# One core, an encoder layer in split float32: the down projection's first weights in other tiles, and planner delays, issue orders and buffers changed at eight other places

## The chip, the cores and the metric

The kernel runs on one core of a Trainium2 chip. The metric is the device time of one execution in microseconds. Three runs of the kernel before took 2294.54, 2300.36 and 2303.19 us; their median, 2300.36 us, is the time before.

## The reference

One layer of a bidirectional encoder is applied to a prompt (1024 tokens) and a sample (256 tokens) with the same weights, D_MODEL 1024, all in float32. In order:

```python
h = rmsnorm(x, norm_mix_w)
proj = h @ w_in                      # q/k/v, decays, gates, gMLP halves
y_a = deltanet_branch(...) @ w_up_a  # conv, gated delta rule in both directions, 4 heads
y_b = spatial_gating_branch(...) @ w_up_b
x = x + (sigmoid(gate_a) * y_a + sigmoid(gate_b) * y_b) @ w_out
x = x + memory_cross_attention(rmsnorm(x), rmsnorm(mem), ...)   # 4 heads, 256 memory tokens
h = rmsnorm(x, norm_ffn_w)
gu = h @ ffn_w_gate_up               # 2 x 2816 columns
x = x + (silu(gu[..., :D_FF]) * gu[..., D_FF:]) @ ffn_w_down
y = rmsnorm(x, final_norm_w)
```

## The kernel before, in words

**Products.** Activations lie with channels on partitions and tokens along the free dimension, in three blocks of 512, 512 and 256 tokens (block 2 is the sample). Each factor is split into a high part (a copy to fp32r, on ScalarE, line 125) and a low part (the rest, a subtraction on VectorE or GpSimd, line 126); `mm3` (line 110) makes of each product three: high·high, high·low, low·high. All matrix products pass line 108, transposes line 121.

**Order of the work.** TensorE's order is that in which the program issues its products. A planner in the class `Trunk` sets it: `K.clock` counts planned nanoseconds (`mm` adds n / 2.4 for n fp32r columns). The main work is a generator that yields after every `mm3` step (three products); at each yield `pump` runs the side generators whose due time has come. A side generator's `yield 2800` means: go on when 2800 ns of planned products have been issued. `K.finish` runs a side generator to its end with no main work between. The other engines' and the DMA queues' orders are made by the tile scheduler, and each queue then runs in order. A tile of a pool with `bufs=n` may exist n times under its tag; a further one waits for the oldest.

**Norms.** `Norm.add` sums squares; `Norm.rest` (line 247) waits `lag`, sums over partitions by products with ones (`nacc`), makes the reciprocal root by eleven small VectorE operations (`nst`, lines 224 to 228, 258), yields 2800, broadcasts the roots over partitions by float32 products with the unit matrix (line 263), and scales the eight 128-channel slices, one per `pace`. Those in `shared` are scaled by ScalarE and multiplied on GpSimd (lines 271, 272). The sample's norm before the FFN takes `lag=LAGS`; the last norms are started by `last_norm` (line 1931), for block 1 after phase 5 of the down projection, for block 0 after phase 6, for the sample at the end.

**Mixer.** `decays` (line 439) computes the decays; after `yield 5000` four products with triangular matrices sum them (line 480). Four heads and the sample are five batches of `dn_batch` (line 648), side work beside the main convolutions, gates and memory projections. A batch solves its triangular systems on VectorE, waits for the previous batch's flags, sums squares of the queries (`SQ`), joins the inverse's blocks by products and transposes (`LEV`), sets the flag "inverse", and scans its chunks (`SC1` to `SC3`). When the last batch is done, `load_ya` (line 1108) loads branch A, with `yield YA` between its six pairs of loads, beside `up_b` (line 1090), whose gate loads go over the same queue.

**Attention.** `load_kv` (line 1344) loads and splits keys and values of a head through one tile `kraw`. `attend` computes scores, exponentials `e` (8 buffers), transposes and outputs.

**FFN.** The up projections of the prompt work by a Strassen-like scheme: `ff_first` (line 1698) is its first of 22 tiles. Its products take the weights `gu_w[0, 0..3]` and the activation quarters b11, b21, r1, b22, r2, t3, t4; the last three are made there on VectorE and ScalarE. `gu_gate(1)` splits the first weight of the next tile, the low part on GpSimd. The sample's products begin with the second tile (`ff_up(1)`).

The down projection of the prompt (`down_prompt`, line 1874) has seven phases of six units (one to two pairs of 128 channels). `a_prep(i)` makes the weight combination of unit i and splits it into a room from `a_room(i)` (line 1648); the rooms rotate over two pairs of the pool `wp` and one tile of the pool `ffd` (`down_room`, line 1821), which is opened only when the up projection's pools are closed. The raw weights of unit u and half e lie at `home[e][u]`; units 1 to 3 of the first phase are loaded early into other tiles, 4 and 5 by the loads of step 0 (line 1861). The unit's 12 or 24 products read the room (`ahl` in `ffd`, `whi`/`wlo` in `wp`) and the activations `bhl`, which are loaded from `gq`, where the up projection stored them.

```python
def a_room(i):
    if i % 3 < 2:
        return tuple(t.rearrange(...) for t in pair_of(wp))
    t = down_room()
    return t[:, 0], t[:, 1]
```

Of the kernel before, what the change touches and what calls it, by code (L numbers as in the profile page):

```python
# [163 lines left out]
def trunk_kernel(ctx: ExitStack, tc: tile.TileContext, a):  # L164
# [65 lines left out]
    class Norm:  # L230
# [16 lines left out]
        def rest(self, xk, wcol, sink, pace=1300, shared=(), lag=1500, ks=range(KT), inplace=False, ready=None, halves=1):  # L247
# [12 lines left out]
            yield 2800  # L260
# [178 lines left out]
    def decays():  # L439
# [37 lines left out]
        yield 5000  # L477
# [170 lines left out]
    def dn_batch(bi, qkv, chains):  # L648
# [175 lines left out]
        for level, mask in enumerate((m64, m128)):  # L824
# [21 lines left out]
            for hs in halves:  # L846
                for q, d in ((lo64, 0), (hi64, 1)):
                    S.activation(Mt[q, hs, :], U[d][q, hs, :], AF.Copy)
                yield LEV
            for hs in halves:  # L850
# [8 lines left out]
        flags.add(("inverse", bi))  # L859

# [334 lines left out]
    class OutProj:  # L1195
# [21 lines left out]
        def run(self, xsrc, scale, wcol, xpool, store, sinks=None, then=None, ready=None):  # L1217
# [23 lines left out]
            for b, (t0, n) in enumerate(BLOCKS):  # L1241
# [15 lines left out]
                if sinks is None or b == 2:  # L1257
                    norm_b = nms[b].rest(xk, wcol, to_h(hs, b), 600, lag=1500 if sinks is None else LAGS, inplace=sinks is not None, ready=ready)
# [20 lines left out]
    def attend(h, qh, ql, kh, kl, vh, vl, o_h):  # L1279
        es = {}  # L1280

        def scores(b, c):
# [12 lines left out]
            e = tp.tile([P, NMEM], F32, tag="e", name="e", bufs=8)  # L1295
# [45 lines left out]
    for h in range(HEADS):  # L1341
        qh, ql = (tq.tile([P, 2, NTOK], F32R, tag=f"q{i}", name=f"q{i}") for i in range(2))

        def load_kv():
            kv = [tp.tile([P, 1024], F32R, tag=f"kv{i}", name=f"kv{i}", bufs=2) for i in range(4)]
            for i, src in enumerate((kd[2 * h : 2 * h + 2], vd[h])):
                raw = tp.tile([P, 1024], F32, tag="kraw", name="kraw")
# [105 lines left out]
    def gu_gate(f):  # L1453
        if f < NFF:
            gu_w[f, 0] = pair_of(wp)
            split(*gu_w[f, 0], gu_raw[f][0], G)
# [63 lines left out]
    split(*gu_w[0, 2], gu_raw[0][0], V)  # L1520
    for k in range(4):
        parts(r2, k, r2_raw[k], V)
    fs = ExitStack()
# [124 lines left out]
    def a_room(i):  # L1648

        if i % 3 < 2:  # L1650
# [47 lines left out]
    def ff_first():  # L1698
# [12 lines left out]
        yield from gu_mm(pe, w(1), 1, r1, True)  # L1711
        make_t3()
        yield from gu_mm(pf, w(2), 1, b22, True)
        gu_gate(1)
        yield from gu_mm(pa, w(1), 0, r2, False)
# [95 lines left out]
    f0 = [hp.tile([P, 4, 1024], F32, tag=t, name="w0") for t in ("hi1",)]  # L1811
    f1 = [hp.tile([P, 4, 1024], F32, tag=t, name="w1") for t in ("lo1",)]
    for n, w in ((4, f0), (4, f1), (2, f0), (2, f1)):
        e = int(w is f1)
        w.append(dpool.tile([P, n, 1024], F32, tag=f"w{e}{n}", name=f"w{e}"))
    for e, w in enumerate((f0, f1)):
        for u in range(1, len(units)):
            home[e][u] = w[(u - 1) // 2], 2 * ((u - 1) % 2)
# [55 lines left out]
    def down_prompt():  # L1874
        a_prep(2)
# [4 lines left out]
        for ph, (key, more, half, b, sign) in enumerate(STEPS):  # L1880
# [20 lines left out]
            for u, pairs in enumerate(units):  # L1901
# [13 lines left out]
                if i == 1:  # L1915
                    pair_home(1)
                    SY.dma_start(home[1][0][0], w_dn[1][:, units[0], :])
                a_prep(i + 3)
# [12 lines left out]
    def last_norm(nm, b):  # L1931
# [5 lines left out]
        K.side(nm.rest(lambda k: x2[b][:, k, :], S_FIN, sink, PACEF, SHARED[b], LAGF[b]))  # L1937
# [84 lines left out]
SQ, EXP, LEV = 1000, 4000, 500  # L2022
SC1, SC2, SC3 = 1200, 700, 700
TAIL, ROOT, FIRST_EXP = 3000, (2500, 2500, 2500, 16000, 2500), 3500
YA = 3000
# [3 lines left out]
LAGS, FIRST_W = 19000, 9000  # L2029
# [83 lines left out]
```

## Time and profile before

| what | value |
|---|---|
| median of three runs | 2300.36 us |
| the profiled execution, its own time | 2304.28 us |
| its span, first to last instruction | 2301.6 us |
| TensorE (PE) busy | 2214.0 us |
| mean granted clock of TensorE | 0.986 |
| VectorE (DVE), ScalarE (ACT), GpSimd (POOL) busy | 1389.9, 815.9, 531.9 us |
| HBM read and written | 182.19 and 78.16 MB |

The profile is of one execution. Its rows name an engine, a line of the kernel, an operation and the tiles written and read (`out<-in`); the part behind `[` or `<-` is idle time of the engine just before, and what ended it. PEclk is the granted clock of TensorE as a share of its full 2.4 GHz. Windows are in us from the start of the span.

### The profile page before, as it was taken

What the parts mean: (1) busy time and instruction counts of PE and PEld (TensorE: products, weight loads), DVE (VectorE), ACT (ScalarE), POOL (GpSimd) and SP (SyncE); (2) the same over time, 40 slices, a digit from 0 to 9 for tenths busy, and PEclk for the clock granted to TensorE, in tenths of its full rate; (3) what the DMA queues carried; (4) which work ended last, traced back from release to release, by engine and by line L of the source; (5) the groups of instructions that cost most, each with busy time, mean ns of one, the idle gap of its engine ahead of it and who ended that gap; (6) DMA issues with size and microseconds to landing.
All of it is one profiled execution on the core that took longest, in us unless ns stands there. A gap on an engine that the chain in (4) does not pass through costs nothing.

```text
span 2301.6 us, 32403 instructions
## 1 busy us (share of the span) xinstructions
PE 2214.0 (96%) x12464; PEld 1929.4 (84%) x12464; DVE 1389.9 (60%) x2773; ACT 815.9 (35%) x1480; POOL 531.9 (23%) x353
## 2 busy tenths in 40 slices
PE   6999999999999999999999999899999999899988
PEld 6988888888888888888888888788888888688888
DVE  7758677787985954564534547543443443477565
ACT  5433242333424433122244423322322323243543
POOL 3010000000000000013231321666666666000220
PEclk9999999999999999999999999999999999999999
DMA  5221322313234545862221431132222223573530
GB/s 184 87 78 58 110 58 85 77 52 107 67 115 116 160 123 200 274 229 92 78 92 60 153 140 65 65 107 87 79 87 74 80 81 108 191 276 132 179 133 19
DMA packets 191301, 262.47 MB, mean 114 GB/s; under 512 B 72410, under 2 KB 102698, under 8 KB 191146
## 3 DMA queue, kind: packets, MB, share of 16 engines
q1 hardware_dynamic: 171306, 231.30, 31.1%
q10 hardware_dynamic: 19840, 29.11, 3.5%
q8 instruction: 97, 1.59, 0.3%
q14 instruction: 58, 0.48, 0.1%
HBM read 182.19 MB, written 78.16 MB: 113 GB/s over the span
## 4 chain that ended last, share of the span: by engine, by line
PE 42%; issue 4%; DVE 2%; DMA 1%; POOL 1%; ACT 1%; POOLq 0%; SPq 0%; ACTq 0%; DVEq 0%
PE bank L108 42%; DMA kraw<-vd 0%; DMA braw<-gq 0%; POOL nacc L244 0%; PE bank L121 0%; DMA gq<-t 0%; DVE wlo L126 0%; POOL kv L126 0%; DMA kraw<-kd 0%; DMA raw<-in_w_dn 0%; POOL x L272 0%; ACT whi L125 0%; ACT nsq L243 0%; DVE x L1528 0%; DVE t4l L126 0%
## 5 line engine op out<-in xcount | busy, mean ns | idle before, releaser
L108 PE MATMUL bank<-hi,whi 128*128 128x512 f32 (+1 forms) x2144 | 765.5, 357 | 0.9 <-ACT whi L125 0.9
L108 PE MATMUL bank<-hi,wlo 128*128 128x512 f32 (+1 forms) x2144 | 750.0, 350 | 3.6 <-POOL wlo L126 2.5
L108 PE MATMUL bank<-lo,whi 128*128 128x512 f32 (+1 forms) x2144 | 749.8, 350 | 0.0
L108 PEld LDWEIGHTS bank<-hi,wlo 128*128 128x128 f32 x2144 | 406.5, 190 | 58.7 <-POOL wlo L126 2.9
L108 PEld LDWEIGHTS bank<-hi,whi 128*128 128x128 f32 x2144 | 407.1, 190 | 50.7 <-ACT whi L125 1.3
L108 PEld LDWEIGHTS bank<-lo,whi 128*128 128x128 f32 x2144 | 407.5, 190 | 48.6 <-issue 0.2
L126 POOL TENSOR_TENSOR wlo<-raw,whi 128x1024 fp32r<-128x1024 f32 x71 | 181.2, 2556 | 440.9 <-ACT whi L125 437.7
L125 ACT ACTIVATE whi<-raw 128x1024 fp32r<-128x1024 f32 (+1 forms) x141 | 144.5, 1025 | 213.9 <-PE bank L108 151.5
L126 POOL TENSOR_TENSOR wlo<-room,whi 128x1024 fp32r<-128x1024 f32 x42 | 101.0, 2405 | 112.1 <-ACT whi L125 110.3
L108 PE MATMUL bank<-bhl,whi 128*128 128x512 f32 x392 | 121.9, 393 | 0.0
L126 DVE TENSOR_TENSOR wlo<-raw,whi 128x1024 fp32r<-128x1024 f32 (+1 forms) x70 | 79.9, 1142 | 50.2 <-ACT whi L125 50.1
L125 ACT ACTIVATE whi<-room 128x1024 fp32r<-128x1024 f32 x42 | 44.6, 1061 | 140.2 <-PE bank L108 140.2
L1777 DVE TENSOR_TENSOR room<-room,bank 128x512 f32<-128x512 f32 x21 | 14.5, 688 | 131.8 <-ACT room L1557 131.8
L108 PE MATMUL bank<-bhl,ahl 128*128 128x512 f32 x336 | 81.3, 398 | 9.6 <-ACT ahl L125 9.6
L591 DVE SCALAR_TENSOR_TENSOR acc<-craw,sm,acc 128x510 f32<-128x510 f32 (+1 forms) x96 | 72.4, 755 | 24.7 <-ACT acc L589 23.5
L108 PEld LDWEIGHTS bank<-bhl,whi 128*128 128x128 f32 x392 | 74.2, 190 | 15.6
L108 PEld LDWEIGHTS bank<-bhl,ahl 128*128 128x128 f32 x336 | 63.9, 191 | 24.5 <-ACT ahl L125 10.0
L126 DVE TENSOR_TENSOR wlo<-w,whi 128x512 fp32r<-128x512 f32 (+1 forms) x59 | 52.4, 890 | 48.0 <-ACT whi L125 47.8
L737 DVE TENSOR_TENSOR W<-W,UT 128x2 f32<-128x2 f32 (+30 forms) x155 | 73.1, 472 | 13.2 <-DMA W<-in_eye 8.6
L243 ACT ACTIVATE nsq<-x 128x512 f32<-128x512 f32 (+1 forms) x70 | 40.4, 584 | 107.4 <-DVE x L1227 93.5
L952 ACT ACTIVATE gs<-bank 128x512 f32<-128x512 f32 (+1 forms) x60 | 31.3, 521 | 131.3 <-PE bank L108 121.6
L108 PE MATMUL bank<-bhl,wlo 128*128 128x512 f32 x196 | 76.9, 392 | 0.0
(326 smaller groups left out, 4200.3 us busy)
## 6 DMA issues: line engine op xcount, KB each, us to landing
raw<-in_w_gu SPq DMA_DIRECT2D x44, 512.0 KB, 3.9
braw<-gq SPq DMA_DIRECT2D x14, 1024.0 KB, 5.6
w<-in_w_dn SPq DMA_DIRECT2D x11, 1024.0 KB, 8.7
raw<-in_w_g SPq DMA_DIRECT2D x20, 512.0 KB, 3.5
gq<-t SPq DMA_DIRECT2D x33, 256.0 KB, 2.0
gtd<-gs ACTq DMA_DIRECT2D x32, 256.0 KB, 2.0
raw<-in_w_qkv SPq DMA_DIRECT2D x12, 512.0 KB, 3.6
gq<-r SPq DMA_DIRECT2D x22, 256.0 KB, 4.3
```

The lines of the kernel that those rows point to most:

```text
L108: self.nc.tensor.matmul(out, l, r, start=start, stop=stop, skip_group_check=more)
L125: self.nc.scalar.activation(hi, src, AF.Copy)
L126: (eng or self.nc.vector).tensor_tensor(out=lo, in0=src, in1=f32(hi), op=ALU.subtract)
L243: S.activation(sq, x, AF.Square)
L591: V.scalar_tensor_tensor(out=dst, in0=src, scalar=wj, in1=dst, op0=ALU.mult, op1=ALU.add)
L737: V.tensor_tensor(out=t3, in0=u3[:, i:, c:].rearrange("p j c -> p c j"), in1=XL[:, 32 * i + i : 32 * i + 32].unsqueeze(1).to_broadcast([P, ...
L952: S.activation(t, ps, AF.Tanh, scale=0.5)
L1777: V.tensor_tensor(out=c22, in0=c22, in1=pe, op=ALU.add)
```

## The change

It puts the first weights of the down projection into other tiles (units 4 and 5 of the first half into the former activation tiles `hi1` and `lo1`), lets the first three units take pairs of `wp` (unit 2 the one that unit 0 leaves, its preparation issued behind unit 0) and unit 3 the tile of `ffd`, so that the rotation goes on with units 6, 9, ... there; gives `Norm.rest` a second delay `lag2`, longer for the sample's norm before the FFN and the prompt's last norms, whose first delay and pace are longer too; reorders the first up tile and moves one split's low part to VectorE; gives `kraw` two buffers and `e` six; adds two delays to the recurrence and lengthens one; lengthens the delay of the decay products and that between branch A's loads.

```diff
@@ Norm.rest
-        def rest(self, xk, wcol, sink, pace=1300, shared=(), lag=1500, ks=range(KT), inplace=False, ready=None, halves=1):
+        def rest(self, xk, wcol, sink, pace=1300, shared=(), lag=1500, ks=range(KT), inplace=False, ready=None, halves=1, lag2=2800):
...
-            yield 2800
+            yield lag2
             pb = bank()
@@ decays
-        yield 5000
+        yield 9000
         pr = bank()
@@ dn_batch
                     S.activation(Mt[q, hs, :], U[d][q, hs, :], AF.Copy)
                 yield LEV
+            yield LEVT
             for hs in halves:
                 pt = bank()
...
         flags.add(("inverse", bi))
+        yield SCAN
@@ OutProj.run
-                    norm_b = nms[b].rest(..., lag=1500 if sinks is None else LAGS, ...)
+                    norm_b = nms[b].rest(..., lag=1500 if sinks is None else LAGS, ..., lag2=2800 if sinks is None else LAGS2)
@@ attend, load_kv
-            e = tp.tile([P, NMEM], F32, tag="e", name="e", bufs=8)
+            e = tp.tile([P, NMEM], F32, tag="e", name="e", bufs=6)
-                raw = tp.tile([P, 1024], F32, tag="kraw", name="kraw")
+                raw = tp.tile([P, 1024], F32, tag="kraw", name="kraw", bufs=2)
@@ FFN, first tile
-    def gu_gate(f):
+    def gu_gate(f, eng=G):
         if f < NFF:
             gu_w[f, 0] = pair_of(wp)
-            split(*gu_w[f, 0], gu_raw[f][0], G)
+            split(*gu_w[f, 0], gu_raw[f][0], eng)
...
-    split(*gu_w[0, 2], gu_raw[0][0], V)
     for k in range(4):
         parts(r2, k, r2_raw[k], V)
+    split(*gu_w[0, 2], gu_raw[0][0], V)
...
         yield from gu_mm(pe, w(1), 1, r1, True)
+        yield from gu_mm(pa, w(1), 0, r2, False)
+        gu_gate(1, V)
         make_t3()
         yield from gu_mm(pf, w(2), 1, b22, True)
-        gu_gate(1)
-        yield from gu_mm(pa, w(1), 0, r2, False)
         u2 = copied(pa, cs[:, 1, :])
@@ down projection
-        if i % 3 < 2:
+        if i % 3 or i < 3:
             return tuple(t.rearrange("p (k c) -> p k c", c=512) for t in pair_of(wp))
...
-    f0 = [hp.tile([P, 4, 1024], F32, tag=t, name="w0") for t in ("hi1",)]
-    f1 = [hp.tile([P, 4, 1024], F32, tag=t, name="w1") for t in ("lo1",)]
-    for n, w in ((4, f0), (4, f1), (2, f0), (2, f1)):
-        e = int(w is f1)
-        w.append(dpool.tile([P, n, 1024], F32, tag=f"w{e}{n}", name=f"w{e}"))
-    for e, w in enumerate((f0, f1)):
-        for u in range(1, len(units)):
-            home[e][u] = w[(u - 1) // 2], 2 * ((u - 1) % 2)
+    def w_tile(p, tag):
+        return p.tile([P, 4, 1024], F32, tag=tag, name=tag)
+
+    wa, wb = w_tile(hp, "hi1"), w_tile(hp, "lo1")
+    wc, wd, we = (w_tile(dpool, f"w{i}") for i in range(3))
+    for e, ts_ in enumerate((((wc, 0), (wc, 2), (wa, 0), (wa, 2), (wb, 0)), ((wd, 0), (wd, 2), (we, 0), (we, 2), (wb, 2)))):
+        home[e].update(enumerate(ts_, 1))
...
     def down_prompt():
-        a_prep(2)
         norms = {}
...
+                if i == 0:
+                    a_prep(2)
                 a_prep(i + 3)
...
-        K.side(nm.rest(..., S_FIN, sink, PACEF, SHARED[b], LAGF[b]))
+        K.side(nm.rest(..., S_FIN, sink, PACEF, SHARED[b], LAGF[b], lag2=LAGF2[b]))
@@ constants
-SQ, EXP, LEV = 1000, 4000, 500
+SQ, EXP, LEV, LEVT, SCAN = 1800, 4000, 500, 1000, 1000
-YA = 3000
+YA = 4500
-LAGS, FIRST_W = 19000, 9000
+LAGS, LAGS2, FIRST_W = 19000, 8000, 9000
-LAG0, LAGF, PACEF = 7500, (3500, 3500, 1500), 500
+LAG0, LAGF, LAGF2, PACEF = 7500, (8000, 6000, 1500), (9000, 9000, 2800), 1000
```

## Rows read from the trace of the kernel before

**Rows 1.** The page, part 1: busy us, share of the span, instructions.

```profile
PE 2214.0 (96%) x12464; PEld 1929.4 (84%) x12464; DVE 1389.9 (60%) x2773; ACT 815.9 (35%) x1480; POOL 531.9 (23%) x353
```

**Rows 2.** Who TensorE waited for: us in total, times, longest us.

```profile
PE bank L108 <- DVE nst L228: 16.0, 7, 4.5
...
PE bank L108 <- ACT ahl L125: 9.6, 1, 9.6
...
PE bank L108 <- DVE U L837: 3.7, 4, 1.2
PE bank L121 <- ACT gb L848: 3.5, 4, 1.9
PE bank L108 <- DVE stage L1102: 3.2, 4, 1.9
...
PE bank L108 <- DVE e L1298: 2.5, 2, 1.6
PE bank L108 <- DVE gm L473: 2.4, 1, 2.4
...
PE bank L108 <- POOL nacc L244: 1.0, 1, 1.0
```

**Rows 3.** Windows, TensorE: length, PE busy (instructions), granted clock, DMA share, GB/s.

```profile
126.00:130.00 4.00, 4.00 (x12) 0.57 0.17 64
282.00:290.00 8.00, 8.00 (x30) 0.57 0.77 155
...
1452.00:1462.00 10.00, 5.86 (x16) 0.66 0.21 80
2000.00:2011.00 11.00, 4.29 (x11) 0.53 1.00 368
2186.00:2191.00 5.00, 4.38 (x17) 0.68 0.34 102
2228.00:2235.00 7.00, 4.92 (x23) 0.55 0.03 10
...
900.00:950.00 50.00, 47.21 (x238) 0.97 0.95 327
```

**Rows 4.** Timeline of TensorE: start, us, operation, tiles, count, [idle before <- releaser].

```profile
281.91 1.02 PE L108 MATMUL bank<-cst,gs 128*128 128x1 f32 x8 [1.36 <-DVE vw L763]
...
894.46 1.04 PE L121 MATMUL bank<-cst,o 128*128 128x128 f32 x8
...
1443.88 0.79 PE L108 MATMUL bank<-hi,wlo 128*128 128x512 f32 x1 [2.48 <-POOL wlo L126]
...
1455.62 1.22 PE L108 MATMUL bank<-cst,nst 128*128 128x128 f32 x4 [4.48 <-DVE nst L228]
...
1465.04 0.28 PE L108 MATMUL bank<-hi,whi 128*128 128x256 f32 x1
...
2006.68 7.66 PE L108 MATMUL bank<-bhl,ahl 128*128 128x512 f32 x24 [9.56 <-ACT ahl L125]
...
2195.05 1.16 PE L108 MATMUL bank<-cst,nst 128*128 128x128 f32 x8 [2.25 <-DVE nst L228]
...
2230.08 2.08 PE L108 MATMUL bank<-cst,nst 128*128 128x128 f32 x8 [3.54 <-DVE nst L228]
```

**Rows 5.** The chain that ended last, in order of time: start, us, what.

```profile
1162.99 4.09 DMA kraw<-vd
...
1998.44 6.94 DMA gq<-t
```

**Rows 6.** Window in the first up tile: busy us (instructions) of PE, PEld, DVE, ACT, POOL.

```profile
1430.00:1455.00 25.00, 16.64 (x65) 12.39 (x63) 23.59 (x42) 11.45 (x19) 3.74 (x2) 0.91 0.18 60
```

**Rows 7.** Timeline of VectorE: the sample's scaled splits, first and last; a down split.

```profile
1456.87 1.65 DVE L276 SCALAR_TENSOR_TENSOR x<-x,sm,bank 128x256 f32<-128x256 f32 x4 [1.31 <-PE bank L108]
...
1462.75 0.76 DVE L126 TENSOR_TENSOR lo<-x,hi 128x256 fp32r<-128x256 f32 x1
...
1997.81 1.21 DVE L126 TENSOR_TENSOR wlo<-araw,whi 128x1024 fp32r<-128x1024 f32 x1
```

More of the change, by code (lines that the diff above doesn't have):

```diff
@@ L1257, in run @@
                 if sinks is None or b == 2:
-                    norm_b = nms[b].rest(xk, wcol, to_h(hs, b), 600, lag=1500 if sinks is None else LAGS, inplace=sinks is not None, ready=ready)
+                    norm_b = nms[b].rest(xk, wcol, to_h(hs, b), 600, lag=1500 if sinks is None else LAGS, inplace=sinks is not None, ready=ready, lag2=2800 if sinks is None else LAGS2)
                 else:
@@ L1935, in sink @@
             (SY if k % 2 else S).dma_start(a["yT"][:, k, t0 : t0 + n], t)
-        K.side(nm.rest(lambda k: x2[b][:, k, :], S_FIN, sink, PACEF, SHARED[b], LAGF[b]))
+        K.side(nm.rest(lambda k: x2[b][:, k, :], S_FIN, sink, PACEF, SHARED[b], LAGF[b], lag2=LAGF2[b]))
     order_s = [2 * p + 1 for p in range(PAIRS)] + [2 * p for p in range(PAIRS)]
```

## The prediction

> **What bounds the kernel now.** I read the page first: TensorE (PE) is busy for 2214.0 of 2301.6 us [rows 1]. So the kernel is bound by PE almost everywhere, and about 88 us are left in which PE stands still. The second view is who PE waited for [rows 2]: the 88 us are many short waits, and the change touches sites that have their own rows there (norm broadcasts, the down projection's weight split, inverse and scan of the recurrence, gate loads, attention, decays). The third view is the granted clock around such waits [rows 3]: behind several of them the clock stands at 0.53 to 0.68 on average over 4 to 11 us, so PE then works partly at 1.2 GHz, and a wait costs more than its own length. I price that as busy time × (1 − clock). The fourth view shows the single waits in time [rows 4].
>
> **What could be had**, site by site (wait + slow clock behind it):
> A decays: 2.4 [rows 2] + 4.00 × 0.43 = 1.7 [rows 3] = 4.1 us.
> B recurrence: query sums 1.4 [rows 4] + 8.00 × 0.43 = 3.4 [rows 3]; transposes of the inverse 3.5, first scan products 3.7 [rows 2]. Together 12.0.
> C gate loads of up_b: 3.2 [rows 2].
> D attention: 2.5 [rows 2].
> E first up tile: 2.48 + 4.48 [rows 4] + 5.86 × 0.34 = 2.0 [rows 3] = 9.0.
> F begin of the down projection: 9.56 [rows 4] + 4.29 × 0.47 = 2.0 [rows 3] = 11.6.
> G last norms of the prompt: 1.0 [rows 2] + 2.25 + 3.54 [rows 4] + 4.38 × 0.32 + 4.92 × 0.45 = 3.6 [rows 3] = 10.4.
> Sum 52.8 us, 2.3% of the span. Nothing is removed from the work of PE, so this is the ceiling.
>
> **Part by part.**
>
> **A.** The wait before the decay products grows from 5000 to 9000 of the planner's ns. The planner counts a 512-column product as 213 ns, so some 4 us of main products move ahead of them. 4 us is more than the 2.4 us they waited; nothing near it needs the result, whose reader waits another 12000 planner ns at least. The four products and two transposes and one store move with it, behind other work. Gain 4.1; low end 1, if VectorE (DVE) is late again.
>
> **B.** SQ + 800 ns twice, LEVT + 1000, SCAN + 1000. Side work is issued only between steps of three products, 0.64 us by the planner, so 1000 means up to two steps or 1.28 us. The four scan waits sum to 3.7 and are at most 1.2 each [rows 2]: covered, I take 3.0. The transposes' longest wait is 1.9 [rows 2], of which some 0.6 remain: 2.9 of 3.5. For the query sums one step of 0.64 covers about half of 1.36: half of 4.8, that is 2.4. Sum 8.3. What it costs: each of the five batches is 2 × 0.8 + 1.0 = 2.6 us longer before the next may start, so the last one ends 5 × 2.6 + 1.0 = 14 us later. The DVE steps of the scan meet other convolution work then; the trace doesn't show that mix, so the low end is 2 and the high end 12.0.
>
> **C.** load_ya now sleeps 4500 instead of 3000 ns between its six pairs of loads, so that it ends 6 × 1.5 = 9 us later than its later start (14 us, from B). Its start is bound to the end of the last batch, whose output transposes stand at 894.46, just as the first up_b products begin [rows 4]. By the planner's count up_b is 8 × (24 × 0.213 + 12 × 0.107) = 51 us of products; the loads ended after some 18 of these and will end after about 41. The cover holds, with 10 us over. DMA engines are busy for 0.95 of 900 to 950 at 327 GB/s [rows 3], so thinning the loads can help the gate loads but pushes bytes into the time of the first merge loads. I take 1, between −4 (a wait like the present one appears later, with some slow clock) and 3.2. The Trainium skill ("DMA: Bandwidth & Descriptors", Issuing engines are not separate DMA queues) says that transfers from all issuing engines interleave on the same 16 engines. By that rule pacing saves no byte and C would be 0, which would move the sum by 1 us; the share of 0.95 agrees with it.
>
> **D.** kraw gets a second buffer. In the chain a value load of 4.09 us is waited for before ScalarE (ACT) can go on to the exponentials queued behind its split [rows 5]; that load started only when the previous split was done with the one buffer. With two it starts a whole load and split earlier, and the wait goes. Exponential tiles fall from 8 to 6: four of a block plus two ahead are in use at most, so I cost that at nothing (cover: the transposes that free them are issued before). Gain 2.5, low end 1.
>
> **E.** Three edits. (1) r2's products come before b22's, so the weight pair that f = 1 waits for is free 12 products earlier, and b22's 12 products cover its split. (2) That split's low half goes from POOL to DVE. The 2.48 us wait [rows 4] goes. But DVE is busy for 23.59 of the 25 us around it [rows 6], so DVE is the bound there and gets 1.2 us more (a 1024-column low half took 1.21 [rows 7]). (3) The sample's norm broadcast comes 8000 instead of 2800 ns behind its sums, so 5 us of products (t3's rest, t4) move ahead of it into the 4.48 us wait. It is then the last thing before the sample's own products, and these need its eight scaled splits, which took from 1456.87 to 1463.51 [rows 7], 6.6 us that t3 and t4 covered before. New order: broadcast at 1455.6 + 1.2 (the added low half), 1.2 for its products [rows 4], then 6.6 to the last split at 1464.6. Before, the sample's products began at 1465.0 [rows 4] and the first 24 of them are 24 × 0.107 = 2.6 by the planner, to 1467.6. Now they end some 0.3 behind the last split, at 1464.9: gain 2.7. Low end −2, high end 9.0.
>
> **F.** Units 0 and 1 end at 2006.68 − 9.56 = 1997.1 [rows 4]. Unit 2's split into the room in the new pool waited for a store to gq, 6.94 us from 1998.44 [rows 5]. Now unit 2 takes the pair that unit 0 leaves, in the place in which unit 3's split stood: DVE done at 1997.81 + 1.21 = 1999.0 [rows 7]. So 1.9 us remain; then 24 products, 24 × 0.213 = 5.1 by the planner, to 2004.1. Unit 3 now takes the late room: the store lands at 2005.4, PE could start on the high half at 2006.68 and needs the low half 1.2 later, so 2007.9. Before, unit 3 began at 2006.68 + 7.66 = 2014.3. Gain 6.4, and as the remaining waits may still pull the clock down for a while, I take 6. The loads of units 4 and 5 go to tiles that the last up products free, so they no longer stand on SP's queue behind a wait for a store; no DMA is added. If those two 512 KB loads get ahead of the stores, the room is later by their time: low end 2. High end 11.6.
>
> **G.** Sums 4.5 and 2.5 us later, broadcasts 6.2 later again, passes spaced 1000 instead of 500. Each is more than its wait (1.0, 2.25, 3.54). Passes, POOL multiplies and eight output DMAs per block, on SP and ACT, come at most 4.5 + 6.2 + 4 = 15 us later. For block 0 they lie in the sample's down projection, which is 528 products of 256 columns, 56 us by the planner, and began only shortly before the present broadcast at 2230.08 [rows 4]; so they don't reach the end. Gain 9.5, low end 6 (DVE late again), high end 10.4. The sample's own last norm keeps its values.
>
> **Sum.** 4.1 + 8.3 + 1 + 2.5 + 2.7 + 6 + 9.5 = 34.1 us. The profiled execution took 2304.28 (span 2301.6), 3.9 above the median of 2300.36; so 2270.2 against its own time, and 2266 against the median, which I predict. Low ends: 1 + 2 − 4 + 1 − 2 + 2 + 6 = 6; high ends 52.8.
>
> **The rivals.**
> (1) Only the placements gain. In E, F and C the next late thing (DVE at 94% [rows 6], the store, the DMA engines) eats the gain, and B gives half: 4.1 + 4 + 2.5 + 8 = 18.6, so 2282. For it: E and F leave new waits by my own working. Against: F's 24 products have nothing that holds them but the split.
> (2) All waits named go: 2300.4 − 52.8 = 2248. For it: most covers exceed their waits. Against: E and F.
> (3) Slower. The one mechanism: the recurrence's end slides past its cover. load_ya is 23 us later (14 + 9); should the last of its loads land behind the end of up_b, PE stands until it is split, and every further us of lateness is a us of the kernel. If all 23 go through, with 5 of slow clock, against low ends elsewhere (10), it is 2318. It decides from 10 us of lateness beyond my count. Against it: 10 us of products to spare.
> (4) The change does not do what it says: the delays are in planner time, and where no main products are left they place nothing. Then nothing moves measurably: 2299. Against it: all but the sample's last norm have main products behind them.
>
> **How the numbers follow.** Forecast 0.61, rival 1 0.22, rival 2 0.09, rival 3 0.03, rival 4 0.05. A measurement of this kernel can tell about 0.5% (11.5 us) from no change. Faster by over 0.5% (under 2288.9): forecast, rival 2 and most of rival 1, 0.87; within 0.5%: 0.09; slower: 0.04. Range 2246 to 2286: from rival 2's time to a little behind rival 1's, since the terms err independently and all low ends at once are unlikely.
>
> **What would show it.** In the changed profile: no wait of the decay product over 0.5 us; scan and inverse rows under 1 us in total each; the broadcasts of the prompt's last norms without a wait and the clock 1.0 near 2190 and 2230; at the down projection two waits of 2 to 3 us in place of 9.56, on ACT or DVE splits; waits of the sample's products on its scaled splits at the end of the first up tile. The forecast is wrong if PE's total idle time stays above 70 us, or if waits on the merge or gate loads grow past 5 us.

## The result, and the profile after

The changed kernel takes 2262.39 us (median of 4 runs, 2260.64 to 2267.29), the kernel before 2299.49 beside it (4 runs, 2294.54 to 2303.19). The ratio is 0.9843 with a 95% interval of 0.9819 to 0.9868: 1.6% faster, or 37.1 us. The prediction was 2266, range 2246 to 2286.

The profiled execution of the changed kernel is the slowest of its four, 2267.29 with a span of 2265.1. The page, part 1 (busy us, share of the span, instructions), answers to [rows 1]:

```profile
PE 2204.3 (97%) x12464; PEld 1923.5 (85%) x12464; DVE 1396.8 (62%) x2774; ACT 815.7 (36%) x1480; POOL 527.5 (23%) x352
```

TensorE (PE) runs the same 12464 products and stands still for 60.8 us of the span, where it was 87.6. It is also busy for 9.7 us less with the same work, because less of it falls under the low clock: busy time × (1 − granted clock), added up over all stretches at the low level, is 24.7 us in the profile of before and 15.6 in this one. Less standing still and less busy time together are the 36.5 us by which the span shrank. Whom PE waited for (us in total, times, longest), beside [rows 2]:

```profile
PE bank L108 <- DVE nst L228: 9.8, 5, 4.0
...
PE bank L108 <- ACT ahl L125: 2.2, 1, 2.2
...
PE bank L108 <- DVE stage L1104: 2.0, 3, 1.1
...
PE bank L108 <- DVE vg L434: 1.3, 1, 1.3
...
PE bank L108 <- DVE ahl L126: 1.1, 1, 1.1
PE bank L121 <- ACT gb L848: 0.9, 1, 0.9
```

The rows of [rows 2] for U (first scan products), e (softmax weights), gm (decays) and for the norm sum that GpSimd adds (nacc) are gone. The wait for ahl, the split weights of the down projection, fell from 9.6 to 3.3 us on two engines, that for gb, of the inverse, from 3.5 to 0.9. New is vg, the normed operand of the spatial gating, and nst is still the largest of these. The timeline of PE (start, us, operation, tiles, count, idle before and its releaser) shows where, to be read beside [rows 4]:

```profile
130.08 1.40 PE L108 MATMUL bank<-sw,vg 128*128 128x128 f32 x6 [1.32 <-DVE vg L434]
...
281.41 1.02 PE L108 MATMUL bank<-cst,gs 128*128 128x1 f32 x8 [1.78 <-DVE vw L763]
...
1437.84 1.22 PE L108 MATMUL bank<-cst,nst 128*128 128x128 f32 x4 [4.02 <-DVE nst L228]
1440.08 0.58 PE L108 MATMUL bank<-hi,whi 128*128 128x256 f32 x1 [1.02 <-ACT hi L125]
...
1441.73 0.58 PE L108 MATMUL bank<-lo,whi 128*128 128x256 f32 x1 [1.06 <-POOL lo L126]
...
1978.11 0.50 PE L108 MATMUL bank<-bhl,wlo 128*128 128x512 f32 x1 [1.29 <-DVE wlo L126]
...
1985.62 0.73 PE L108 MATMUL bank<-bhl,ahl 128*128 128x512 f32 x2 [2.23 <-ACT ahl L125]
...
1987.45 6.67 PE L108 MATMUL bank<-bhl,ahl 128*128 128x512 f32 x22 [1.10 <-DVE ahl L126]
...
2173.53 1.05 PE L108 MATMUL bank<-cst,nst 128*128 128x128 f32 x8
...
2208.42 1.05 PE L108 MATMUL bank<-cst,nst 128*128 128x128 f32 x8
```

The prompt's last two broadcasts (2173.53, 2208.42) wait for nothing now. The down projection has three short waits where it had 9.56. The first up tile still has its wait on the sample's broadcast, 4.02 for 4.48, and two more behind it. Windows of the same profile, with the columns of [rows 3] and the other engines between:

```profile
282.00:290.00 8.00, 8.00 (x29) 6.73 (x30) 1.16 (x2) 0.00 (x0) 0.00 (x0) 0.61 0.71 141
1436.00:1444.00 8.00, 4.08 (x15) 3.49 (x16) 6.60 (x16) 4.27 (x9) 6.81 (x6) 0.59 0.42 131
...
2186.00:2191.00 5.00, 4.80 (x33) 4.08 (x32) 4.32 (x7) 4.70 (x9) 3.86 (x3) 1.00 0.33 109
2228.00:2235.00 7.00, 7.00 (x61) 7.00 (x59) 3.26 (x6) 3.16 (x5) 0.00 (x0) 1.00 0.00 1
```

The figure behind the busy times of the five engines is the granted clock: 1.00 in the last two, but 0.61 still at 282 and 0.59 in the first up tile.

**Where the time came from, by stage.** Single executions of one kernel lie up to 6.7 us (after) and 8.7 us (before) apart, so the experiments below are read by stages: the time from one product to another in PE's timeline, which leaves the other stages out. The six stages run (1) from the norm broadcast near 103 us to the first product with `acc` (the convolutions' sums); (2) from the first transpose of `acc` to the first key-query product, with the whole recurrence and the gate loads in it; (3) from there to the first norm sum behind the attention; (4) from there to the first product of the down projection, with the first up tile; (5) from there to the first down product of the sample; (6) from there to the last norm broadcast. The 58.7 us between (1) and (2) are the same in all profiles. For the changed kernel stage 3 lies between these two lines of the timeline, 1350.56 − 1138.37 = 212.19:

```profile
1138.37 1.57 PE L108 MATMUL bank<-kv,q 128*128 128x256 f32 x12
...
1350.56 0.95 PE L108 MATMUL bank<-cst,nacc 128*128 128x1 f32 x8
```

All stages of all profiles, in us, made in this way (an asterisk: a part of that stage is undone or altered):

| kernel | 1 | 2 | 3 | 4 | 5 | 6 |
|---|---|---|---|---|---|---|
| before | 112.81 | 882.18 | 216.77 | 615.47 | 229.15 | 76.10 |
| e9, before again | 112.83 | 878.27 | 218.31 | 614.89 | 229.29 | 75.92 |
| after | 111.02 | 865.60 | 212.19 | 617.49 | 218.66 | 70.88 |
| e1 | 112.62 | 863.89 | 212.19 | 617.20* | 219.91 | 70.96 |
| e2 | 112.34 | 860.64 | 212.29 | 615.49* | 220.71 | 70.84 |
| e3 | 110.99 | 876.66* | 212.28 | 616.50 | 220.47 | 70.96 |
| e4 | 112.31 | 865.65* | 212.28 | 617.23 | 218.75 | 71.00 |
| e5 | 111.00 | 860.98 | 212.25 | 616.22 | 225.46* | 69.84* |
| e6 | 111.00 | 861.19 | 212.20 | 616.10 | 222.95* | 73.18* |
| e7 | 111.00 | 860.46 | 218.26* | 616.64 | 220.66 | 70.83 |
| e8 | 111.02 | 862.19* | 212.20 | 617.50 | 220.63 | 70.99 |
| e10 | 111.01 | 866.64* | 212.26 | 616.52 | 220.46 | 71.01 |
| e11 | 110.99 | 861.83 | 212.21 | 620.91* | 218.50 | 70.98 |
| e12 | 111.00 | 862.12 | 212.24 | 617.31* | 219.05 | 70.82 |
| mean without asterisk, after to e12 | 111.4 | 862.1 | 212.2 | 616.8 | 219.8 | 70.9 |

Against the mean of the two profiles of before, the stages give 1.5, 18.1, 5.3, −1.6, 9.4 and 5.1 us, together 37.8.

### The profile page after: what moved, and what is told of

Same layout as the page of the kernel before. It is cut to its first block, busy times and chain, and to the rows that moved or that the text cites. A ratio compares the mean times of both kernels' runs of the same rounds, so it can differ in the third digit from the quotient of the medians.

```text
span 2265.1 us, 32398 instructions
## 1 busy us (share of the span) xinstructions
PE 2204.3 (97%) x12464; PEld 1923.5 (85%) x12464; DVE 1396.8 (62%) x2774; ACT 815.7 (36%) x1480; POOL 527.5 (23%) x352
## 4 chain that ended last, share of the span: by engine, by line
PE 79%; DVE 9%; DMA 4%; issue 4%; ACT 2%; POOL 1%; SPq 0%; ACTq 0%; POOLq 0%; DVEq 0%
PE bank L108 78%; DMA tbd<-stage 1%; PE bank L121 1%; DVE acc L591 1%; DVE wlo L126 1%; DVE W L737 1%; DMA braw<-gq 1%; DVE nt L276 0%; DVE sw L895 0%; DVE W L740 0%; DMA gb<-grd 0%; DVE U L837 0%; DMA t<-sgd 0%; DVE lo L126 0%; DMA stage<-gtd 0%
## 5 line engine op out<-in xcount | busy, mean ns | idle before, releaser
L108 PE MATMUL bank<-bhl,whi 128*128 128x512 f32 x456 | 140.6, 389 | 0.0
L108 PEld LDWEIGHTS bank<-bhl,whi 128*128 128x128 f32 x456 | 85.5, 188 | 17.8
L108 PE MATMUL bank<-bhl,wlo 128*128 128x512 f32 x228 | 88.8, 390 | 1.3 <-DVE wlo L126 1.3
L243 ACT ACTIVATE nsq<-x 128x512 f32<-128x512 f32 (+1 forms) x70 | 40.2, 584 | 102.4 <-DVE x L1229 91.1
L244 DVE TENSOR_TENSOR nacc<-nacc,nsq 128x512 f32<-128x512 f32 (+1 forms) x73 | 55.3, 758 | 34.0 <-ACT nsq L243 32.8
L1581 DVE SCALAR_TENSOR_TENSOR t<-bank,t 128x512 f32<-128x512 f32 (+1 forms) x44 | 24.5, 558 | 81.9 <-PE bank L108 81.9
L857 POOL COPY UT<-U 64x512 f32<-64x512 f32 x20 | 13.8, 697 | 246.7 <-PE bank L108 245.1
```

The source lines that it names most:

```text
L108: self.nc.tensor.matmul(out, l, r, start=start, stop=stop, skip_group_check=more)
L243: S.activation(sq, x, AF.Square)
L244: (eng or V).tensor_tensor(out=self.acc, in0=self.acc, in1=sq, op=ALU.add)
L857: G.tensor_copy(Um[q, hs, :], U[d][q, hs, :])
L1581: V.scalar_tensor_tensor(out=out, in0=u, scalar=sign, in1=t, op0=ALU.mult, op1=ALU.mult)
```

## The experiments

All but the last were timed once, with a profile; e9 is the kernel before, the others are the changed kernel with one edit.

**e1, the order of the first up tile as before** (E).

```
+    split(*gu_w[0, 2], gu_raw[0][0], V)
     for k in range(4):
         parts(r2, k, r2_raw[k], V)
-    split(*gu_w[0, 2], gu_raw[0][0], V)
...
-        yield from gu_mm(pa, w(1), 0, r2, False)
-        gu_gate(1, V)
         make_t3()
         yield from gu_mm(pf, w(2), 1, b22, True)
+        gu_gate(1)
+        yield from gu_mm(pa, w(1), 0, r2, False)
```

> The changed kernel with the old order of the first up tile (split of the third weight pair first, b22 before r2, low half of the next tile's gate weight on GpSimd), the late broadcast of the sample's norm kept. In the changed kernel the second tile's r2 products start at 1452.9 us. Theory (VectorE's work sets this stretch, order on TensorE is free): the second tile's r2 starts within 1.5 us of that, and the time is within 2 us of the changed kernel's 2262. Rival (the new order gained some 6 us, and the late broadcast lost 8): r2 starts 4 us or more later, the time is 4 to 7 us more.

2267.01 us, which is above what the theory named, but so are most of the single executions below, and the profiled one of after. Stage 4 took 617.20, within what the changed order gives (616.10 to 617.50). The wait of 2.43 us on GpSimd's low half is back in this profile, and the broadcast waits less by 1.5 (2.53 for 4.02): no worth of the order shows in this run, as the theory had it.

**e2, the sample's second lag as before** (E).

```
-LAGS, LAGS2, FIRST_W = 19000, 8000, 9000
+LAGS, LAGS2, FIRST_W = 19000, 2800, 9000
```

> The changed kernel with the sample's broadcast 2800 instead of 8000 planner ns behind its sums, new order kept. Theory (the late broadcast is the loss: eight scaled splits behind it are no longer covered by the products of t3 and t4): TensorE waits some 4 to 6 us before the broadcast, ahead of t3, and not for the scaled splits; the second tile's r2 starts 3 to 5 us earlier than 1452.9, and the time is 2258. Rival (VectorE's chain of small operations sets the broadcast wherever it is put, and what it covers is only moved): r2 within 1.5 us of 1452.9.

2264.68 us. The second tile begins at 1448.60, 4.3 us earlier than in after, but 2.3 of these lie ahead of the stage. Stage 4 is 1.3 us under the mean and 2.0 under after, 615.49, as long as before the change (615.47, 614.89). That is less than the theory's 3 to 5 us, and it does not show that the lag of 8000 is what costs E its time: PE's waits from the begin of the stage to the second tile add up to 10.6 us in e2 and to 8.8 to 11.6 (mean 10.6) in the eight profiles with the changed code there. What e2 has less of is the low clock in that stretch: busy time × (1 − granted clock) is 3.1 us against 2.3 to 6.1 (mean 4.3), and it changes from execution to execution of the same code. What the lag does change is the form of the wait. In e2 (PE):

```profile
1430.11 1.22 PE L108 MATMUL bank<-cst,nst 128*128 128x128 f32 x4 [5.75 <-DVE nst L228]
```

The wait is longer, but the sample's scaled splits behind it are then done beside the products of t3 and t4. In the changed kernel the norm's chain of eleven small VectorE operations, of 0.15 to 0.17 us each, was strung out between large ones (VectorE, after):

```profile
1428.84 0.16 DVE L258 TENSOR_SCALAR bank<-bank 128x2 f32<-128x2 f32 x1
...
1431.46 1.68 DVE L1581 SCALAR_TENSOR_TENSOR room<-room,t 128x512 f32<-128x512 f32 x1
...
1436.04 1.67 DVE L1595 TENSOR_TENSOR r<-t,room 128x512 f32<-128x512 f32 x1
1437.64 0.15 DVE L228 SCALAR_TENSOR_TENSOR nst<-bank,nst 128x2 f32<-128x2 f32 x1
```

It took 8.8 us from the first to the last; in e2 it took 3.4 (1426.50 to 1429.89), as in the kernel before (1452.03 to 1455.40).

**e3 and e4, the recurrence's waits and the query sums as before** (B).

```
-SQ, EXP, LEV, LEVT, SCAN = 1800, 4000, 500, 1000, 1000
+SQ, EXP, LEV, LEVT, SCAN = 1000, 4000, 500, 0, 0      # e3
+SQ, EXP, LEV, LEVT, SCAN = 1000, 4000, 500, 1000, 1000  # e4
```

> The changed kernel without the recurrence's three delays (query sums 1000 again, the two new yields at 0). Theory (the delays gained more than was predicted, because they also end waits of the sample's scan and of the memory projection's splits): the first products of branch A's up projection, at 936.5 us in the changed kernel, start 12 to 15 us later, waits for the inverse's transposes and first scan products sum to over 6 us again, the time is 2274 to 2278. Rival (8.3 us, as predicted): they start 7 to 10 us later, time 2270 to 2272.

> The changed kernel with the query sums' delay at 1000 again, the other two delays kept. Theory (the wait before the query sums is set by the end of VectorE's triangular solve, so placing them later on TensorE gains nothing): the wait near 281 us grows by what TensorE saved before, and the scan of every batch starts at the same time within 1 us; the time is within 2 us of 2262. Rival (a third of the recurrence's gain is from this delay, as predicted): 2 to 4 us more.

e3: 2279.61 us; the first product of branch A's up projection comes 12.8 us later than in after (949.25 in place of 936.46), and stage 2 is 876.66, 14.6 over the mean. Whom PE waited for from 285 to 950 us, first in e3, then in e1, whose recurrence is that of the changed kernel:

```profile
PE bank L108 <- DVE sw L895: 5.9, 11, 1.8
PE bank L108 <- DVE stage L1104: 4.7, 4, 1.9
PE bank L108 <- DVE U L837: 3.9, 4, 1.1
PE bank L121 <- ACT gb L848: 3.6, 4, 1.9
PE bank L108 <- DVE wlo L126: 1.9, 2, 1.1
```

```profile
PE bank L108 <- DVE sw L895: 4.6, 12, 0.9
PE bank L108 <- DVE stage L1104: 3.6, 5, 1.1
...
PE bank L121 <- ACT gb L848: 0.9, 1, 0.9
```

All rows of these two answers sum to 23.7 and 12.5 us. U and gb make 6.6 of the 11.2 between them; the rest are sites that the change does not touch, such as wlo, the splits of the memory projection's weights. The theory holds, though the time is 1.6 us above what it named; its rival falls. e4: 2268.93 us, stage 2 865.65. That is 3.5 over the mean; after itself has 865.60, but with 3.1 us of low clock at 282 that e4 has not, and the next longest of the same code is 1.8 under e4 (e1, 863.89). So the query sums alone are worth 2 to 3.5 us at best. The wait near 281 that they were priced on does not follow the delay: it is 1.01 us in e4 and 0.95 in e3, and between nothing (e2, e5) and 1.78 (after) in the profiles with the longer delay.

**e10, the yield ahead of the scan taken out** (B).

```
-SQ, EXP, LEV, LEVT, SCAN = 1800, 4000, 500, 1000, 1000
+SQ, EXP, LEV, LEVT, SCAN = 1800, 4000, 500, 1000, 0
```

> The changed kernel with the yield of 1000 ahead of the scan taken out, and the one ahead of the inverse's transposes kept. Undoing both (with the query sums) cost 13 us to the memory output's first product, and the query sums alone 2.2. Theory A (each yield carries its own wait: the inverse's transposes behind ScalarE's copies, the first scan products behind the last inverse level on VectorE): 3 to 5 us later at the first product of the memory output, waits on U rows back at about 1 us in four of the five blocks, and no wait on gb of more than 1 us. Theory B (the yields work by delay alone, so that one of them lets the other work follow): within 1.5 us.

2268.83 us; stage 2 is 4.5 us over the mean. Whom PE waited for, from 100 us on:

```profile
PE bank L108 <- DVE U L837: 4.8, 4, 1.7
...
PE bank L121 <- ACT gb L848: 0.9, 1, 0.9
```

U is back four times, gb is not: the yield ahead of the scan carries U's wait, and gb's is left to the other. No run took out that other one alone.

**e5, the begin of the down projection as before** (F: the old homes of the weight tiles, the old room of unit 2, `a_prep(2)` at the start).

```
-        if i % 3 or i < 3:
+        if i % 3 < 2:
...
-                if i == 0:
-                    a_prep(2)
```

> The changed kernel with the begin of the down projection as before: the old homes of the weight tiles, the old room for unit 2's split and a_prep(2) at the start of the stage. My theory (the stage gained because its second unit no longer waits for a transfer that the up stage's last stores hold up): TensorE's waits in the first 40 us of the down projection rise from 4.6 us (1.29 + 2.23 + 1.10) to 8 to 10.5 us in one wait, with one more stretch at the low clock behind it, and from the stage's first product to the sample's first one the stage is 4 to 6 us longer than the 218.7 us of the changed kernel. Rival (the transfer was late in before only because the up stage ended as it then did, so that the old begin costs nothing now): waits below 6 us and the stage within 1.5 us of 218.7.

2267.24 us; stage 5 is 5.7 us over the mean and 6.8 over after. In the waits from the stage's first product on, one row stands for the three of after:

```profile
PE bank L108 <- ACT ahl L125: 9.7, 1, 9.7
```

The theory holds, with 6.8 us a little above the 4 to 6 that it named. Stage 6 is 1.1 us shorter in this run, so the old begin costs 4.6 us in stages 5 and 6 together. In the changed kernel's profile the next late thing is the second load of the second operand: issued at 1975.14, when the splits of the first have freed its buffer, ScalarE takes it up at 1981.67.

**e6, the prompt's last norms as before** (G).

```
-LAG0, LAGF, LAGF2, PACEF = 7500, (8000, 6000, 1500), (9000, 9000, 2800), 1000
+LAG0, LAGF, LAGF2, PACEF = 7500, (3500, 3500, 1500), (2800, 2800, 2800), 500
```

> The changed kernel with the prompt's last two norms paced and broadcast as before (lags 3500, 3500, steps of 500, second lag 2800). My theory: TensorE again waits 2 to 2.5 us and 3 to 3.6 us for the column sums of the two norms, about 1 us for a norm sum of GpSimd's, and works at the low clock for some microseconds behind each; from the stage's first product to the sample's last down product the stage is 9 to 11 us longer than in the changed kernel. Rival (the waits alone count and the clock falls elsewhere anyway): 5.5 to 7 us longer.

2267.90 us; stages 5 and 6 are 3.17 and 2.25 over their means, 5.4 together. That is the rival's number, nearly: the waits came back, the clock did not fall. The timeline's rows and the windows behind them (granted clock 1.00; 0.68 and 0.55 in [rows 3]):

```profile
2162.39 1.16 PE L108 MATMUL bank<-cst,nst 128*128 128x128 f32 x8 [2.74 <-DVE nst L228]
...
2196.92 1.16 PE L108 MATMUL bank<-cst,nst 128*128 128x128 f32 x8 [2.45 <-DVE nst L228]
```

```profile
2162.00:2168.00 6.00, 5.61 (x29) 4.78 (x30) 6.00 (x9) 2.16 (x4) 3.68 (x3) 1.00 0.33 122
2196.00:2203.00 7.00, 6.08 (x51) 6.08 (x52) 4.92 (x10) 1.86 (x3) 4.15 (x3) 1.00 0.37 139
```

**e7, the attention's buffers as before** (D).

```
-            e = tp.tile(..., bufs=6)
+            e = tp.tile(..., bufs=8)
-                raw = tp.tile(..., name="kraw", bufs=2)
+                raw = tp.tile(..., name="kraw")
```

> The changed kernel with one buffer for the attention's raw keys and values and eight for the weights of the softmax, as before. My theory (the second buffer lets the next load go out before GpSimd has split the one before): from the first query-key product to the attention's last norm sum it takes 216 to 217.5 us again, against 212.2 in the changed kernel, the loss in the first 25 us of the stage, and a wait of TensorE on a split key or value tile of 3 us or more. Rival (the stage gained because it began earlier against its loads, or from the smaller number of softmax buffers): 212 to 213.5 us.

2268.01 us; stage 3 is 218.26, 6.0 over the others. The time is the theory's and somewhat more; the tile it waits for is another, the weights of the softmax and not a split. PE, then ScalarE (ACT) of e7:

```profile
1141.25 2.50 PE L108 MATMUL bank<-kv,q 128*128 128x256 f32 x12 [3.17 <-DVE e L1300]
```

```profile
1136.77 1.06 ACT L125 ACTIVATE kv<-kraw 128x1024 fp32r<-128x1024 f32 x1 [7.25 <-DMA kraw<-kd]
...
1139.91 0.45 ACT L1298 ACTIVATE bank<-bank,st 128x256 f32<-128x256 f32 x1 [0.87 <-ACT q L1359]
```

ScalarE waits for the raw load and has the exponentials behind its split. That is the prediction's mechanism, and not the one of this run's theory. The run undoes two edits at once; no run kept the second raw buffer with eight softmax buffers, so that their smaller number adds nothing is argued from these rows only.

**e8, the pace of the gate loads as before** (C): `YA = 3000` for 4500.

> The changed kernel with the load of the recurrence's output paced at 3000 per step as before, not 4500. My theory (the wider pace spreads six loads and six VectorE steps so that the memory projection's own splits and stores are not pushed back): the first up product comes 1 to 3 us later, with waits of TensorE on the staged output of 2 us or more at one place where the changed kernel shows 1.1 and 0.8. Rival (the pace does nothing and those waits went because the recurrence ends earlier): within 0.7 us.

2264.81 us; stage 2 took 862.19, the mean is 862.1. The rival holds: the pace is worth nothing that shows, and the same code spreads from 860.46 to 865.60 there.

**e9, the kernel before once more.**

> The kernel of before, unchanged, profiled a second time: how much of its time is the low clock behind waits, and does it fall at the same places? Undoing the prompt's last norms alone cost 5.3 us, by its waits alone, where the two kernels differ by 10 to 11 us over the same stretch, in which the profile of before also had low-clock windows at 2186 and 2230. Theory A (whether the clock falls behind a wait of 2 to 3.5 us is settled anew in each execution): the waits come back within 0.3 us each, but at least two of the low-clock stretches at 126, 282, 452, 866, 1452, 2186 and 2230 are missing, and the span differs from 2301.6 by the clock time lost less. Theory B (the clock follows from the order of the work alone): the low-clock stretches stand at the same places, within 2 us.

2300.76 us, span 2298.7. Its windows:

```profile
282.00:290.00 8.00, 8.00 (x31) 6.80 (x31) 1.54 (x3) 0.39 (x1) 0.00 (x0) 0.60 0.75 155
452.00:460.00 8.00, 7.58 (x57) 7.19 (x58) 7.28 (x13) 3.12 (x7) 0.51 (x2) 1.00 0.52 180
1165.00:1172.00 7.00, 5.50 (x26) 4.74 (x27) 6.17 (x18) 3.87 (x13) 1.79 (x1) 0.76 0.22 75
...
2183.00:2191.00 8.00, 6.09 (x30) 4.54 (x28) 7.25 (x15) 4.04 (x7) 2.37 (x2) 1.00 0.41 119
2225.00:2233.00 8.00, 5.76 (x28) 5.76 (x29) 4.80 (x10) 1.98 (x4) 2.91 (x3) 0.57 0.13 49
```

Most of the long waits are the same to 0.3 us (the last broadcasts' 2.25 again and 3.39 for 3.54, the down projection's 9.9 for 9.6); the sample's broadcast in the first up tile is not, 3.23 for 4.48. The low clock behind the waits is not the same either: it is missing at 452 (0.79 from 452 to 460 in the first profile), at 918 and at 2186 (0.68 in [rows 3]), it is there at 1165, where the first profile has none, and it is kept at 126, 282, 866, 1452, 2000 and 2230. Theory A holds by its measure of two places, though not for every wait, and theory B falls; but most places stay.

**e11 and e12, the sample's norm issued elsewhere** (E).

```
-LAGS, LAGS2, FIRST_W = 19000, 8000, 9000
+LAGS, LAGS2, FIRST_W = 15000, 9000, 9000   # e11
+LAGS, LAGS2, FIRST_W = 19000, 5000, 9000   # e12
```

> The changed kernel with the sample's last norm issued earlier, LAGS 15000 and LAGS2 9000 in place of 19000 and 8000, so that its chain of ten small VectorE operations stands ahead of the up stage's large ones and not between them. Theory (the wait of 4.02 us of the broadcast and the 1.02 and 1.06 us of the sample's splits behind it come from that interleaving): the broadcast waits under 1.5 us, and from the attention's last norm sum to the second tile's first product it takes 97 to 100 us, against 102.4 in the changed kernel. Rival (VectorE is full over the whole stretch, so that what is put ahead delays the splits of the first tile by as much): 101.5 to 104 us, with waits on the tile's splits in place of it.

> The changed kernel with LAGS2 5000, between the 8000 of the change and the 2800 of before: the broadcast's products stand behind nine of the twelve products on the third operand's split instead of ahead of them all (2800) or behind the fourth operand's too (8000), and VectorE's chain is not broken by the room sums. Theory (the broadcast has a ready time set by VectorE, and the products ahead of it only fill the wait): it waits 3 to 4 us in place of 5.75 (LAGS2 2800) and 4.02 (8000), without the 1.02 and 1.06 us on the sample's splits behind it, and from the attention's last norm sum to the second tile's first product it takes 98 to 100 us, against 100.4 (2800) and 102.4 (8000); the median is 2258 to 2262 us. Rival (what is saved ahead of the sample's products comes back as a wait on their splits): 100 to 102 us, and a median within 1.5 us of 2262.4.

e11: 2266.71 us, stage 4 620.91, 4.1 over the mean. The broadcast no longer waits, but its norm sum does, 7.85 us behind VectorE. From the begin of the stage to the second tile it took 105.8 us, more than the theory and the rival named: what is put ahead on a full VectorE delays the tile by more than it saves, which is the rival's mechanism. e12: 2264.24 us (5 runs, 2261.31 to 2266.09), ratio to before 0.9837 (0.9822 to 0.9853); the changed kernel's own is 0.9843. The stretch to the second tile took 102.2 us (102.4 in after) and the median is 1.8 above 2262.4: both a little outside what the rival named, and far from the theory. Stage 4 is 617.31. What the rival said holds in kind: the broadcast waits 3.01 us as foreseen, but what is saved there comes back, not on the sample's splits but on t4's products:

```profile
1430.25 0.71 PE L108 MATMUL bank<-cst,nst 128*128 128x128 f32 x4 [3.01 <-DVE nst L228]
...
1436.38 0.79 PE L108 MATMUL bank<-t4h,whi 128*128 128x512 f32 x1 [4.72 <-ACT room L1559]
```

```profile
1434.48 1.06 ACT L125 ACTIVATE whi<-room 128x1024 fp32r<-128x1024 f32 x1 [2.55 <-POOL room L1478]
...
1435.75 0.58 ACT L1559 ACTIVATE room<-bank 128x512 f32<-128x512 f32 x1
```

The copy that t4's products wait for stood on ScalarE behind a weight split that waited for GpSimd's sums. No version tried is measurably faster than the changed kernel.

## Why the prediction was right, point by point

The sum was 34.1 us and 37.1 came. Two terms missed by more than 4 us, in opposite directions. That the sum came so close is in part luck: by the figures below B and D gave 8.3 to 9.9 us more than their terms, A, C, E and F together 9.0 less.

- **A, 4.1 forecast, 1.8 in most profiles** (stage 1: 112.8 to 111.0; 0.2 to 0.5 in e1, e2 and e4, where the clock fell behind the new wait, 0.81 from 129 to 133 in e1). The decay products wait no longer, as forecast. The step that failed: "nothing near it needs the result" looked at the moved products alone. With them out of the way the main work moves forward, and with it a weight split on GpSimd, from 131.99 us to 127.19. Beside it one of VectorE's passes over vg took 2.58 us in place of 0.54, and PE waited 1.32 us for it. All twelve profiles of the changed code have such a pass (2.57 to 2.58), the two of before have none; no run undid this delay alone. The passes over vg (min, median and max in ns, before, then after) and the split (after):

```profile
L434 DVE TENSOR_SCALAR vg<-vg,sums x10: 528/538/546, 53.1 to 128.3; 128x512 f32<-128x512 f32 x10
```

```profile
L434 DVE TENSOR_SCALAR vg<-vg,sums x10: 534/546/2576, 53.0 to 130.4; 128x512 f32<-128x512 f32 x10
...
127.19 2.55 POOL L126 TENSOR_TENSOR wlo<-raw,whi 128x1024 fp32r<-128x1024 f32 x1 [3.14 <-ACT whi L125]
```

- **B, 8.3 forecast, 14.6 measured** (e3). The mechanism stood: the inverse and scan rows of [rows 2] are at 0.9 and nothing, and e10 shows one yield with one wait. The mis-sized step is the list of what could be had: it held the gs wait and the U and gb rows, while 4.6 of the 11.2 us between e3 and e1 lay in waits of other sites in the same stretch. Query sums: 2.4 were priced on the wait near 281, which does not follow the delay (e4). The 3.5 us by which stage 2 gained more than e3 took back lie within what the low clock took: busy time × (1 − granted clock) there is 8.5 and 5.1 us in the two profiles of before, 3.4 of it at 282 in both, and 1.7 in e3. At 282 the clock is low in both profiles of before and in one of twelve of the changed code; e3 has none there either, so what of the change removed it, or whether it did, stays open.
- **C, 1 forecast, nothing found** (e8), which lies inside the spread of the stage.
- **D, 2.5 forecast, 4.5 to 6.1 measured** (stage 3; e7). The mechanism was right; the mis-sized term took one of two rows of waits. The transposes waited for e too (before):

```profile
PE bank L121 <- DVE e L1298: 1.1, 1, 1.1
```

  A low clock goes with the waits in e7 and e9 (1165 above), not in the first profile of before.
- **E, 2.7 forecast, −1.6 measured.** The failed step: "broadcast at 1455.6 + 1.2", which let the broadcast be ready when it was, plus one operation. Eleven small VectorE operations whose result is not needed until later were mixed with large ones, and their end moved with the broadcast: it came 87.3 us behind the begin of stage 4 (1437.84 − 1350.56), where it had come 82.3 us behind it in the kernel before and the forecast put it at 83.5. PE's waits up to the second tile add up to 10.6 us on average, where they were 9.8 and 8.8. The low end, −2, came about by that, and the forecast waits on the scaled splits (1.02, 1.06) came on top.
- **F, 6 forecast, 5.7 measured in stage 5, 4.6 with stage 6** (e5). The forecast left waits of 1.9 and, for unit 3, of 3.8 (2007.9 − 2004.1); 1.29, 2.23 and 1.10 came. ScalarE and VectorE are late with ahl there behind the splits of the second operand, whose load is the late thing, not the store.
- **G, 9.5 forecast, 9.9 by the stages** (9.4 + 5.1 in stages 5 and 6, less F's 4.6), of which e6 shows 5.4. The waits went as forecast. The low clock behind the last of them went too, 2.2 and 2.5 us in the two profiles of before (4.92 × 0.45, 5.76 × 0.43), but e6 has the waits without it, so it stays open whether the longer delays removed it.

Rival 1 (placements only, 2282) held for E and C, but not for F, and B gave more than its whole term. Rival 2 (all waits go, 2248) fell with E and with the new waits of A and F, rival 4 (nothing moves) with the stages. Rival 3's late end of the recurrence did not show: the waits for `stage`, the staged output of branch A, are 2.0 us in after and 3.6 in e1, where they were 3.2. PE's idle time is 60.8, under the 70 that would have spoken against the forecast.

## What to carry to other kernels

In this kernel a yield between a producer and its reader was worth the wait it covers where other work was there and the producer's engine had room (B, G); on the full VectorE of the first up tile every lag tried gave 615.5 us, as before the change, or more. A wait on one in-order engine is a wait of everything behind it: in e7 and e12 PE waited 3.17 and 4.72 us for results of operations on ScalarE that stood behind a split with a late input and did not need that input. Work that moves forward can disturb what it now runs beside (A). A site's cost is found by undoing it and timing its stage, not by its own row: B's rows made 6.6 of 11.2 us of waits.

## What the runs showed of the hardware

**The low clock behind a wait comes and goes.** Behind the wait near 281 PE worked for 8 us at a mean granted clock of 0.61 in after and at 1.00 in e1 and e6, which have the same code up to there and waits of 1.78, 1.62 and 1.48 us; the two levels are 1.2 and 2.4 GHz. Both profiles of before have it there (0.57, 0.60). 8.00 × 0.39 makes 3.1 us, of the 4.9 by which the profiled execution of the changed kernel (2267.29) lies above the median. The four executions have mean granted clocks of 0.991, 0.992, 0.993 and 0.994 and times of 2267.29, 2262.83, 2261.95 and 2260.64 us in the same order: 0.003 of 2265 us is 6.8 us, and the times lie 6.7 apart. The Trainium skill ("TensorE: Matmul & The Clock Gate", Part 1: The HAM clock gate) calls the count of slow products at a kernel's start variable from run to run, because the hardware's watch on activity is not tied to the kernel; the traces here agree (near 27 us, ahead of every changed site, the clock is low for a while in nine of the fourteen profiles and not in five) and show it in the middle of a kernel too: 7.38 × 0.21 = 1.5 us at 452 in one execution of before and none in the other, 3.1 us at 282.

**VectorE held up while GpSimd adds.** In after, L1581 and L1595 took 1.68 and 1.67 us while GpSimd added weights (1431.30 to 1437.17), where the same forms took 0.69 with GpSimd standing still (1947.23 and 1947.95); in e12 a low half of 256 columns took 2.39 us for 0.42, beside a split of GpSimd's from 1435.61 to 1437.98. The Trainium skill ("SBUF — State Buffer", Who interferes with whom) says that a VectorE instruction with two inputs in SBUF and a GpSimd instruction that reads SBUF share a read port, and the later one waits for the whole of the other. The rows agree: in e12 the half ended at 1438.26, 0.28 behind GpSimd's. About 2 of the 8.8 us of E's chain are of this kind, by these two rows, and the long pass over vg beside a split of GpSimd's (A) is a like case; no run took GpSimd's work away, so what it costs the kernel is not shown.
